# A hybrid decoder step in fp32: the last up pair's stores and difference through GpSimd, and the order of the first down loads

## The chip, the cores and the metric

One core of a Trainium2 chip runs the whole program in one launch. Its engines are TensorE (PE), VectorE (DVE), ScalarE (ACT), GpSimd (POOL) and SyncE (SP), which issues the DMAs. The metric is device time in microseconds; the kernel before has a median of 2629.21 us over 3 runs (2625.51 to 2635.08).

## The reference

One layer of a decoder trunk for 2048 prompt tokens and 64 sample tokens at width 1024: a mixer (gated DeltaNet heads beside sliding-window attention), and then the gated ConvFFN, of which only the end matters here:

```python
h = _rmsnorm(x, norm_ffn_w[i]) * (1 + sc2) + sh2
u = jnp.einsum('bld,df->blf', h, ffn_w_up[i])            # 1024 -> 2 x 2816
u_c, n_f_buf = _causal_dwconv(u, f_buf, ffn_conv_w[i])   # 3 taps along the tokens
gate, up = jnp.split(u_c + ffn_conv_b[i], 2, axis=-1)
x = x + g2 * jnp.einsum('blf,fd->bld', jax.nn.silu(gate) * up, ffn_w_down[i])
...
y = _rmsnorm(x, final_norm_w)
```

All of it is fp32. The results are the normed tokens and the states.

## The kernel before

A product in fp32 is done as three matmuls on halves: each operand is split into a high part (a cast on ACT) and a low part (a subtraction on DVE), and high x high, high x low and low x high are added up in PSUM. So every weight tile and every token tile costs a load, a cast and a subtraction before PE can use it. In the names, `wr` is a raw weight tile, `wh` and `wl` its parts; `th` and `tl` are the parts of a token tile.

**The end of up.** The 2816 gate and up rows are 22 pairs of 128. Pairs 3 to 20 of the second token half run as quarter products in `up_quarters`, and the last, pair 21 (`p == MI - 1`), as plain products at its end. For each pair `elementwise` convolves the gate (`conv`: one pass of ACT, then taps on DVE), takes the Silu on ACT, convolves the up rows, multiplies on DVE into `act` (L1589) and stores it to `act_d` (L1590). `diff_loads` reads an earlier token half back into `d12`, printed as `d`; `diffs` subtracts it from `act` on DVE (L1504), copies the 64 sample columns on ACT (L1521), and stores the result to `E_d` (L1522), all on SP's queue. The last pair's `act`, `d` and stores are the last things that up does.

**Down.** `down_phase` splits 2816 and 1024 and the tokens in two each and makes seven products of sums (`DOWN`), once for each of two column ranges, 14 in all, numbered q. A product has 11 steps i; a step is 4 blocks of output rows by 3 matmuls of 512 columns, 12 matmuls. For each step `get_w` loads, casts and subtracts a weight tile, and `get_t` does it for a token tile. The tokens of product 0 are sums that lie in DRAM (`T1_d`, loaded into the tiles `cT1_i`, which the profile prints as `cT` and the order below as `cT_i`); those of product 1 are `cB`. Product 0 starts while up's last pair is still in its elementwise work.

`ahead` works through the steps in order, some steps in front of PE: `AHEAD` = 3 as a rule, up to `DR` = 6 near the end of a product. `RAWS` = 4 raw weight tiles and `DR` = 6 split ones go round. The last three steps of a product are done block by block, and each block is then added to the residual tile x (`out`), which `load_x` fetches from `x2T` (L1857) at step 1 and, if there are two, at step 5, behind the load that was issued last (`tc.issue_after(fetched[0])`).

What sets the order: the program is recorded, and a scheduler then fixes one order for each engine by its own simulated times, subject to data, memory and `issue_after`. At run time each engine and each queue goes through its list strictly in order. All DMAs of the kernel before stand in SP's list, so a store that waits for DVE holds up every load behind it. SP's DMAs take eight semaphores in turn, and one is issued only when the eighth before it has landed.

Of the kernel before, what the change touches and what calls it, by code (L numbers as in the profile page):

```python
# [18 lines left out]
ALU = mybir.AluOpType  # L19
# [13 lines left out]
MI = 22  # L33
# [9 lines left out]
LH = L // 2  # L43
# [51 lines left out]
def kernel(  # L95
# [5 lines left out]
    nc = tc.nc  # L101
# [8 lines left out]
    def scratch(name, shape):  # L110
        return dp.tile(shape, F32, tag=name, name=name)
# [5 lines left out]
    act_d = scratch("act_d", [MI, P, LT])  # L117
    ws_d = scratch("ws_d", [2 * KH, P, D])
    ts_d = {t: scratch(f"{t}_d", [KH, P, n]) for t, n in (("T1", LT - LH), ("T3", LH), ("E", LT - LH))}
# [274 lines left out]
    def rest(steps):  # L394
        for _ in steps:
            pass
# [1086 lines left out]
    def up_quarters(first, q, h, W, uc, us, pq, sums_done):  # L1483


        c0 = HALVES[1][0][0]
# [4 lines left out]
        sg, act = [hold(t, [P, n]) for t in ("sgq", "actq")]  # L1491
# [4 lines left out]
        d12, d22 = [hold(t, [P, n]) for t in ("d12", "d22")]  # L1496
# [6 lines left out]
        def diffs(p):  # L1503
            sub = lambda out, a, b: nc.vector.tensor_tensor(out[:, :LH], a[:, :LH], b[:, :LH], ALU.subtract)  # L1504
            if p in K1:
                i = K1.index(p)
                sub(sg, d22, d12)
                nc.sync.dma_start(ts_d["T3"][i], sg[:, :LH])
                yield
                yield  # L1510
                sub(d12, d12, act)
                nc.scalar.mul(d12[:, LH:], act[:, LH:], -1.0)
                nc.sync.dma_start(ts_d["T1"][i], d12)
                yield
                return
            i = K2.index(p)
            more = K2[8:][i:i + 1]
            for k in more:
                nc.sync.dma_start(sg, act_d[k, :, c0:])
            sub(d12, act, d12)  # L1520
            nc.scalar.copy(d12[:, LH:], act[:, LH:])  # L1521
            nc.sync.dma_start(ts_d["E"][i], d12)  # L1522
            yield
            yield
            for k in more:
                sub(sg, sg, d22)
                nc.sync.dma_start(ts_d["E"][i + 8], sg)
            yield
# [7 lines left out]
        def conv(m, rb):  # L1536

            w, st = uc["cw"][:, m], b8(o[:, m, 2:18])
            d = pq.tile([P, 3 * 512], F32, tag="cq", name="cq", bufs=1)[:, :n]
            sb = us.tile([P, NB_S, 2 + NT_S], F32, tag="sbq", name="sbq", bufs=2)  # L1540
            tap = lambda out, src, j: nc.vector.scalar_tensor_tensor(out, src, w[:, j:j + 1], out, ALU.mult, ALU.add)
            nc.scalar.copy(rb[:, 0:2], o[:, m, 0:2])
            nc.scalar.activation(d, rb[:, 2:], AF.Identity, bias=uc["cb"][:, m:m + 1], scale=w[:, 2:3])
            nc.gpsimd.tensor_copy(sb[:, :, :2], st)
            nc.scalar.copy(sb[:, :, 2:], b8(rb[:, 2 + np_:]))
            yield d
            tap(d[:, :np_], rb[:, :np_], 0)
            yield
            tap(d[:, :np_], rb[:, 1:1 + np_], 1)
            for j in range(2):  # L1550
                tap(b8(d[:, np_:]), sb[:, :, j:j + NT_S], j)
            nc.scalar.copy(o[:, m, 0:2], rb[:, np_:np_ + 2])
            nc.gpsimd.tensor_copy(st, sb[:, :, NT_S:])
            yield
# [18 lines left out]
        def elementwise(p, ru, rg):  # L1573

            cg = conv(2 * p, rg)
            dg = next(cg)
            yield
            next(cg)
            yield
            next(cg)  # L1580
            nc.scalar.activation(sg, dg, AF.Silu)
            yield
            cu = conv(2 * p + 1, ru)
            du = next(cu)
            yield
            next(cu)
            yield
            next(cu)
            nc.vector.scalar_tensor_tensor(act, du, 2.0, sg, ALU.mult, ALU.mult)  # L1589
            nc.sync.dma_start(act_d[p, :, c0:], act)  # L1590
            yield

        for j in range(RING_T, RING):
# [31 lines left out]
        p = MI - 1  # L1625
        ru, rg = rbs[0][p % 2], rbs[1][0]
        for i, (rb, tags) in enumerate(((rg, "bgc"), (ru, "aub"))):
# [8 lines left out]
            if not i:  # L1636
# [3 lines left out]
                late = elementwise(p, ru, rg)  # L1640
        rest(late)
        rest(diffs(p))


# [30 lines left out]
    def down_phase(ds, dr, pd):  # L1675
# [12 lines left out]
        def w_src(q, i):  # L1688
            t = DOWN[q % ND][0]
            if t[0] == "A":  # L1690
                return I["w_downT"][(K1, K2)[t[2] == "2"][i]][:, (low, high)[t[1] == "2"]]
            return ws_d[KH * (t in ("S1", "S4")) + i, :, (low, high)[t in ("S1", "S3")]]

        def t_src(q, name, i, r):

            at, g = PW * (q // ND), 2 if name in ("B22", "T3") else 1
            if name[0] == "B":
                at += LH * (g == 1)
                return act_d[(K1, K2)[name[1] == "2"][i], :, at + r.start:at + r.stop]
            return ts_d[name][i, :, at + r.start:at + r.stop]  # L1700

        fetched = []

        def load(tag, src, n, most, bufs):

            raw = (ds if tag in IN_DS else dr).tile([P, most], F32, tag=tag, name=tag, bufs=bufs)[:, :n]
            fetched[:] = [nc.sync.dma_start(raw, src).ins]
            return raw

        def halves(pool, tag, raw, most, bufs):  # L1710
            n = raw.shape[1]
            h, l = [pool.tile([P, most], F32R, tag=f"{tag}{s}", name=f"{tag}{s}", bufs=bufs)[:, :n] for s in "hl"]
            nc.scalar.copy(h, raw)  # L1713
            nc.vector.tensor_tensor(l, raw, h.bitcast(F32), ALU.subtract)  # L1714
            return h, l
# [4 lines left out]
        def get_w(q, i):  # L1720
            if (q, i) not in w:
                raw = load("wr", w_src(q, i), D // 2, D // 2, RAWS)
                stay = q == Q - 1 and i >= DR
                w[q, i] = halves(*((dr, f"w{i}") if stay else (ds, "w")), raw, D // 2, 1 if stay else DR)

        def get_t(q, i, r):

            if (q, i, r.start) in t:
                return
            name = DOWN[q % ND][1]  # L1730
            n = r.stop - r.start
            if name in ("T1", "B22"):
                m = wide(q, 1) if name == "T1" else PW
                held[name, i] = load(f"c{name}_{i}", t_src(q, name, i, slice(0, m)), m, big if name == "T1" else PW, 1)
                raw = held[name, i][:, r]
            elif name == "T2":
                raw = dr.tile([P, big], F32, tag="tr", name="tr", bufs=RAWS)[:, :n]
                nc.vector.tensor_tensor(raw[:, :PW], held["B22", i], held["T1", i][:, :PW], ALU.subtract)
                if n > PW:
                    nc.scalar.mul(raw[:, PW:], held["T1", i][:, PW:], -1.0)  # L1740
            else:
                raw = load("tr", t_src(q, "E" if name == "T4" else name, i, r), n, big, RAWS)
                if name == "T4":
                    nc.vector.tensor_tensor(raw, raw, held["T1", i][:, r], ALU.add)
            t[q, i, r.start] = halves(ds, "t", raw, big, DR)
# [12 lines left out]
        def ahead(f):  # L1758

            while done[0] <= min(f, len(queue) - 1):  # L1760
                q, i, r = queue[done[0]]
                get_w(q, i)
                get_t(q, i, r)
                done[0] += 1
# [37 lines left out]
        for q in range(Q):  # L1802
# [61 lines left out]
            for s in (1, 0) if last else (None,):  # L1864
                f = place[q, 0, subs[s].start] if last else f
                cs = [c for c in order if s is None or c[1] == s]
                for i in range(one):
                    ahead(f + reach(i))
                    products(i, cs)
                    if finish and i:  # L1870
                        next(finish, None)
                    if i in (1, 5):
                        load_x()
                    if q == Q - 2 and i >= 2 and i - 2 + DR < KH:
                        get_w(Q - 1, i - 2 + DR)
                ahead(f + one - 1 + DR)
                for c in cs:
                    for i in range(one, KH):
                        products(i, [c])
                    out(*c)  # L1880
                if last:
                    rest(finish or ())
                    r = subs[s]
                    finish = norm(1, r.start, r.stop - r.start, x, sums[1], cols[1], [acc[0, 1], acc[1, 1]], True)
# [13 lines left out]
    SIDE, DR, RAWS, AHEAD = 3, 6, 4, 3  # L1898
# [17 lines left out]
    with ExitStack() as main:  # L1916
# [169 lines left out]
        with ExitStack() as es:  # L2086
            tq = new_pool(es, "tq", side="right")
            W = Quarters(tq)
            q = token_quarters(h, tq)
# [17 lines left out]
    with ExitStack() as es:  # L2107
        ds = new_pool(es, "ds", side="right")
        dr = new_pool(es, "dr")
        down_phase(ds, dr, new_pool(es, "pd", space=PSUM))  # L2110
# [94 lines left out]
```

## Time and profile before

| | |
|---|---|
| median of 3 runs | 2629.21 us (2625.51 to 2635.08) |
| the profiled execution | 2624.72 us |
| its span | 2622.9 us |
| mean granted clock of TensorE in it | 0.996 |
| DMA | 427.62 MB, all on one queue, mean 163 GB/s |
| down phase in the profile | from 2152.67 us to the end |

A group's row reads: line, engine, operation, written tile <- read tiles, shape, count, then behind the bar the busy time and the mean of one in ns, and behind the second bar the idle time of the engine just before these instructions with what ended it. A row of a timeline begins with start and duration in us; in brackets stands the idle time before it. `SPq` is a DMA issue in SP's queue. A row of the windows gives, for one stretch, its length, the busy time of PE, its weight loads, DVE, ACT and POOL with their counts, then the granted clock, the busy share of the DMA engines and GB/s. In the chain of waits each row is start, duration, and what the end of the program hung on in that time.

### The profile page before, as it was taken

How to read it: one execution, taken by the hardware profiler on the slowest of the kernel's cores; microseconds unless marked ns; L12 is line 12 of the kernel's file. 1: busy time of each engine (PE TensorE's matmuls, PEld its weight loads, DVE VectorE, ACT ScalarE, POOL GpSimd, SP SyncE). 2: the span in 40 equal slices, each digit the busy share in tenths (PEclk: the TensorE clock that was granted, in tenths of full speed). 3: DMA queues.
4: the chain of work that ended last, by engine and by line, in shares of the span. 5: the costliest groups of instructions: out<-in, count | busy, mean ns of one | idle time of the engine just before them, and what ended most of it. 6: DMA issues, size and time to landing. Idle time of an engine off the chain costs nothing.

```text
span 2622.9 us, 45390 instructions
## 1 busy us (share of the span) xinstructions
PE 2553.1 (97%) x16424; PEld 2216.3 (84%) x16424; DVE 1840.1 (70%) x3633; ACT 1288.9 (49%) x3140; POOL 795.7 (30%) x708
## 2 busy tenths in 40 slices
PE   6999999999999999999999999999999999999998
PEld 5677888888888787777877789999999997888998
DVE  6475579896544687788768665886777675687676
ACT  5464365554343455555544353654555554454453
POOL 2064143334232322233121123345565520022022
PEclk9999999999999999999999999999999999999999
DMA  7787554343556353333345266325555447676454
GB/s 274 252 296 270 155 144 120 98 121 83 125 187 204 116 136 90 106 103 90 85 141 203 95 209 222 116 73 166 169 168 180 167 162 273 210 243 201 144 192 135
DMA packets 315820, 427.62 MB, mean 163 GB/s; under 512 B 82211, under 2 KB 206212, under 8 KB 315332
## 3 DMA queue, kind: packets, MB, share of 16 engines
q1 hardware_dynamic: 315596, 424.73, 50.9%
q8 instruction: 129, 2.11, 0.3%
q14 instruction: 95, 0.78, 0.1%
HBM read 305.07 MB, written 120.57 MB: 162 GB/s over the span
## 4 chain that ended last, share of the span: by engine, by line
PE 74%; DVE 10%; DMA 7%; ACT 3%; issue 2%; POOL 2%; SPq 1%; POOLq 0%; DVEq 0%; ACTq 0%
PE up_ps L365 17%; PE dn_ps L1825 16%; PE in_ps L365 12%; PE op_ps L365 5%; PE uq_b L1611 5%; PE uq_c L1611 2%; PE uq_u L1611 2%; PE uq_g L1611 2%; PE pv_ps L1033 1%; DVE ev L573 1%; PE uq_a L1611 1%; DMA mt<-mixd 1%; PE as_ps L996 1%; PE u_ps L811 1%; DVE w_lo L357 1%
## 5 line engine op out<-in xcount | busy, mean ns | idle before, releaser
L365 PE MATMUL in_ps<-hi,w_hi 128*128 128x512 f32 (+2 forms) x880 | 318.1, 364 | 4.7 <-DVE ev L629 2.1
L365 PE MATMUL in_ps<-lo,w_hi 128*128 128x512 f32 (+2 forms) x880 | 314.7, 358 | 1.5 <-DVE lo L297 1.1
L365 PE MATMUL up_ps<-hi,w_hi 128*128 128x512 f32 (+2 forms) x808 | 314.3, 389 | 1.5 <-ACT sg L568 1.5
L365 PE MATMUL up_ps<-lo,w_hi 128*128 128x512 f32 (+2 forms) x808 | 313.5, 388 | 1.9 <-DVE lo L297 1.9
L365 PE MATMUL in_ps<-hi,w_lo 128*128 128x512 f32 (+2 forms) x880 | 314.7, 358 | 0.0
L365 PE MATMUL up_ps<-hi,w_lo 128*128 128x512 f32 (+2 forms) x808 | 311.6, 386 | 0.1
L1825 PE MATMUL dn_ps<-th,wh 128*128 128x512 f32 (+2 forms) x796 | 271.4, 343 | 5.1 <-ACT th L1713 5.1
L1825 PE MATMUL dn_ps<-tl,wh 128*128 128x512 f32 (+2 forms) x796 | 272.6, 343 | 0.0
L1825 PE MATMUL dn_ps<-th,wl 128*128 128x512 f32 (+2 forms) x796 | 271.1, 342 | 0.0
L357 DVE TENSOR_TENSOR w_lo<-w_raw,w_hi 128x1024 fp32r<-128x1024 f32 x115 | 145.2, 1263 | 87.4 <-ACT w_hi L356 82.5
L356 ACT CAST w_hi<-w_raw 128x1024 fp32r<-128x1024 f32 x126 | 132.0, 1048 | 139.6 <-PE op_ps L365 52.5
L365 PEld LDWEIGHTS in_ps<-hi,w_hi 128*128 128x128 f32 x880 | 165.4, 189 | 30.8 <-issue 8.6
L365 PEld LDWEIGHTS in_ps<-lo,w_hi 128*128 128x128 f32 x880 | 166.0, 189 | 21.2 <-issue 3.8
L365 PEld LDWEIGHTS up_ps<-lo,w_hi 128*128 128x128 f32 x808 | 152.3, 188 | 37.4 <-issue 10.7
L365 PEld LDWEIGHTS up_ps<-hi,w_hi 128*128 128x128 f32 x808 | 152.3, 188 | 35.9 <-issue 8.6
L365 PEld LDWEIGHTS in_ps<-hi,w_lo 128*128 128x128 f32 x880 | 165.8, 188 | 17.8 <-issue 3.6
L365 PEld LDWEIGHTS up_ps<-hi,w_lo 128*128 128x128 f32 x808 | 152.1, 188 | 31.5 <-issue 5.3
L1713 ACT CAST wh<-wr 128x512 fp32r<-128x512 f32 x149 | 92.2, 619 | 165.2 <-PE dn_ps L1825 110.0
L1825 PEld LDWEIGHTS dn_ps<-th,wh 128*128 128x128 f32 x796 | 150.9, 190 | 21.1 <-ACT th L1713 5.5
L573 DVE SCALAR_TENSOR_TENSOR ev<-rb,cw,ev 128x512 f32<-128x512 f32 (+2 forms) x180 | 140.3, 785 | 38.6 <-ACT ev L566 36.9
L1825 PEld LDWEIGHTS dn_ps<-tl,wh 128*128 128x128 f32 x796 | 151.0, 190 | 16.1 <-DVE tl L1714 0.4
L1825 PEld LDWEIGHTS dn_ps<-th,wl 128*128 128x128 f32 x796 | 151.1, 190 | 15.4
(565 smaller groups left out, 6514.3 us busy)
## 6 DMA issues: line engine op xcount, KB each, us to landing
w_raw<-in_w_upT_dram SPq DMA_DIRECT2D x50, 512.0 KB
wada<-in_w_ada_dram SPq DMA_DIRECT2D x48, 512.0 KB
w_raw<-in_w_inT_dram SPq DMA_DIRECT2D x44, 512.0 KB
wr<-ws_d SPq DMA_DIRECT2D x88, 256.0 KB
w_raw<-in_w_outT_dram SPq DMA_DIRECT2D x34, 512.0 KB
d<-act_d SPq DMA_DIRECT2D x33, 512.0 KB
wr<-in_w_downT_dram SPq DMA_DIRECT2D x66, 256.0 KB
proj<-ev SPq DMA_DIRECT2D x44, 256.0 KB
```

The lines of the kernel that those rows point to most:

```text
L356: nc.scalar.copy(hi, raw)
L357: (eng or nc.vector).tensor_tensor(lo, raw, hi.bitcast(F32), ALU.subtract)
L365: nc.tensor.matmul(ps[:, :n], a[:, k, :], b[:, k, :n], start=first is not False and k == ks[0] and i == 0, stop=last is not False and k == ...
L573: nc.vector.scalar_tensor_tensor(out, src(j), w[:, j:j + 1], out, ALU.mult, ALU.add)
L811: mm = lambda out, a, b, r, c: nc.tensor.matmul(out, a, b, start=True, stop=True, tile_position=(r, c))
L996: nc.tensor.matmul(banks[v][:, 256 * g:256 * g + 256 - P * k0], qs[:, 2 * (g0 + g) + v], t[:, v, :2 - k0].rearrange("p w j -> p (w j)"), s ...
L1033: nc.tensor.matmul(pv_ps[64 * v:64 * v + 64, :], (vprev[0], vt)[half][:, 64 * v:64 * v + 64], PT[v, half], start=half == k0, stop=half == 1)
L1611: nc.tensor.matmul(bk[t][:, :nb], u[:, k], v[:, k], start=new and k == 0 and y == 0, stop=k == KG - 1 and y == 2, skip_group_check=True)
L1713: nc.scalar.copy(h, raw)
L1825: nc.tensor.matmul(acc[m, s][:, :n], w[q, i][a][:, c], th[b][:, v], start=new and i == 0 and y == 0, stop=i == KH - 1 and y == 2, skip_gro ...
```

## The change

```diff
@@ diffs(p), pairs of K2
             for k in more:
                 nc.sync.dma_start(sg, act_d[k, :, c0:])
+            if p == MI - 1:
+                nc.gpsimd.tensor_tensor(d12[:, :LH], act[:, :LH], d12[:, :LH], ALU.subtract)
+                nc.gpsimd.tensor_copy(d12[:, LH:], act[:, LH:])
+                nc.gpsimd.dma_start(ts_d["E"][i], d12)
+                return
             sub(d12, act, d12)
             nc.scalar.copy(d12[:, LH:], act[:, LH:])
             nc.sync.dma_start(ts_d["E"][i], d12)
@@ elementwise
-            nc.sync.dma_start(act_d[p, :, c0:], act)
+            (nc.gpsimd if p == MI - 1 else nc.sync).dma_start(act_d[p, :, c0:], act)
@@ ahead(f)
                 q, i, r = queue[done[0]]
+                if q == 0 and i >= DR:
+                    get_t(q, i, r)
+                    with tc.issue_after(fetched[0]):
+                        get_w(q, i)
                 get_w(q, i)
                 get_t(q, i, r)
@@ the loop over a product's steps
-                    if i in (1, 5):
+                    if i in ((1, 5) if q else (5,)):
                         load_x()
```

For the last pair the two stores (128x1088 fp32 each, 557 KB), the difference (128x1024) and the copy (128x64) go from SP, DVE and ACT to POOL. For product 0 the weight loads from step 6 on are issued behind the token load of their step, and the residual tile is fetched at step 5 instead of step 1. The calls of `get_w` and `get_t` that follow in `ahead` find these tiles made and do nothing.

The scheduler's order of SP around the end of up, before, from the fourth token tile on (`cT_i` is the token tile of step i of product 0, `wr` a weight tile, `x` the residual tile):

```order
L1707 DMA cT_3_22506<-T_d 128x512
L1707 DMA wr<-ws_d 128x512 x6
L1590 DMA act_d<-actq 128x1088
L1522 DMA E_d<-d_18602 128x1088
L2106 DMA out_ffn_conv_dram<-vout 128x684
L1501 DMA d_18602<-act_d 128x1024
L1590 DMA act_d<-actq 128x1088
L1522 DMA E_d<-d_18602 128x1088
L1707 DMA cT_4_22530<-T_d 128x512
L1857 DMA x_22548<-x2T 128x4x512
L1707 DMA cT_5_22556<-T_d 128x512
L1707 DMA cT_6_22580<-T_d 128x512
```

and now:

```order
L1712 DMA cT_3_22506<-T_d 128x512
L1712 DMA wr<-ws_d 128x512 x2
L1595 DMA act_d<-actq 128x1088
L1527 DMA E_d<-d_18602 128x1088
L2115 DMA out_ffn_conv_dram<-vout 128x684
L1501 DMA d_18602<-act_d 128x1024
L1712 DMA cT_4_22530<-T_d 128x512
L1712 DMA cT_5_22554<-T_d 128x512
L1712 DMA cT_6_22572<-T_d 128x512
L1712 DMA wr<-ws_d 128x512
L1712 DMA cT_7_22596<-T_d 128x512
L1712 DMA wr<-ws_d 128x512
```

The second `act_d` and `E_d` stores, those of the last pair, are gone from SP; four of the six weight loads in a row have moved behind tokens 6 to 9, and x behind the weights of step 9. The stores stand in POOL's order now, behind its last copies of up; its next rows are sums of squares of down's products:

```order
L1549 COPY sbq<-vout 128x8x2
L1558 COPY vout<-sbq 128x16
L1595 DMA act_d<-actq 128x1088
L1521 TENSOR_TENSOR d_18602<-actq,d_18602 128x1024
L1522 COPY d_18602<-actq 128x64
L1523 DMA E_d<-d_18602 128x1088
L1301 TENSOR_TENSOR dsum_23548<-dsum_23548,sq 128x512 x7
```

They are the first DMAs of the program on POOL. The tile of the fourth residual load lies where `act` was, so that load now waits for POOL's first store.

DVE, from the last pair's convolution of the up rows on, before:

```order
L1541 SCALAR_TENSOR_TENSOR cq<-sbq,vcw,cq 128x64 x2
L1589 SCALAR_TENSOR_TENSOR actq<-cq,sgq 128x1088
L1504 TENSOR_TENSOR d_18602<-actq,d_18602 128x1024
L1714 TENSOR_TENSOR wl<-wr,wh 128x512
L1714 TENSOR_TENSOR tl<-cT_4_22530,th 128x512
L1714 TENSOR_TENSOR wl<-wr,wh 128x512
L1714 TENSOR_TENSOR tl<-cT_5_22556,th 128x512
```

and now:

```order
L1546 SCALAR_TENSOR_TENSOR cq<-sbq,vcw,cq 128x64 x2
L1594 SCALAR_TENSOR_TENSOR actq<-cq,sgq 128x1088
L1719 TENSOR_TENSOR tl<-cT_4_22530,th 128x512
L1719 TENSOR_TENSOR tl<-cT_5_22554,th 128x512
L1719 TENSOR_TENSOR tl<-cT_6_22572,th 128x512
L1719 TENSOR_TENSOR wl<-wr,wh 128x512
L1719 TENSOR_TENSOR tl<-cT_7_22596,th 128x512
```

The difference and the weights of step 6 no longer stand between the last product and `tl` of step 4.

PE at step 4 of product 0, with the tiles' numbers (22532 and 22533 are `th` and `tl` of step 4, the `dn_ps` are the four blocks), before:

```order
L1825 MATMUL dn_ps_22459<-th_22532,wh_22526 128x512
L1825 MATMUL dn_ps_22459<-tl_22533,wh_22526 128x512
L1825 MATMUL dn_ps_22459<-th_22532,wl_22527 128x512
L1825 MATMUL dn_ps_22460<-th_22532,wh_22526 128x512
L1825 MATMUL dn_ps_22460<-tl_22533,wh_22526 128x512
L1825 MATMUL dn_ps_22460<-th_22532,wl_22527 128x512
```

and now:

```order
L1834 MATMUL dn_ps_22459<-th_22532,wh_22526 128x512
L1834 MATMUL dn_ps_22460<-th_22532,wh_22526 128x512
L1834 MATMUL dn_ps_22458<-th_22532,wh_22526 128x512
L1834 MATMUL dn_ps_22457<-th_22532,wh_22526 128x512
L1834 MATMUL dn_ps_22459<-tl_22533,wh_22526 128x512
L1834 MATMUL dn_ps_22459<-th_22532,wl_22527 128x512
```

The four matmuls that need only `th` now come first, so `tl` is asked for four matmuls into the step; the other steps keep the old order.

## The prediction

> **What bounds the kernel now.** I read the page first, then who TensorE (PE) waits for, the chain that ended last, and the timelines around the one large wait.
>
> ```profile
> span 2622.9 us, 45390 instructions
> ...
> PE 2553.1 (97%) x16424; PEld 2216.3 (84%) x16424; DVE 1840.1 (70%) x3633; ACT 1288.9 (49%) x3140; POOL 795.7 (30%) x708
> ...
> L1825 PE MATMUL dn_ps<-th,wh 128*128 128x512 f32 (+2 forms) x796 | 271.4, 343 | 5.1 <-ACT th L1713 5.1
> ```
>
> PE is busy for 97% of the span, so an edit gains only where PE stands still. The down projection's matmuls (L1825) have one idle time, 5.1 us, ended by a cast of ACT. The profiled execution took 2624.72 us, 1.8 us more than its span, and lies 4.5 us below the median of the runs shown, 2629.21 us. I work out the sum against it and take the difference over to the median.
>
> The chain of waits says what led up to that cast (start, us, what):
>
> ```profile
> 2161.66 1.30 DVE actq L1589
> ...
> 2162.98 1.24 DVE d L1504
> ...
> 2164.27 0.32 SPq L1522
> ...
> 2164.68 3.46 DMA cT<-T_d
> ...
> 2168.17 0.63 ACT th L1713
> ...
> 2168.84 31.21 PE dn_ps L1825 x124
> ```
>
> The load of down's fifth token tile (step 4, cT) was asked for only at 2164.68, when the last up pair's product was done on DVE (2162.96), its difference too (2164.22), and SP had issued the store of that (2164.27). SP's own timeline shows the order:
>
> ```profile
> 2137.98 8.27 SPq L1707 DMA_DIRECT2D wr<-ws_d  x6
> ...
> 2152.36 0.32 SPq L1522 DMA_DIRECT2D E_d<-d  x1
> 2153.99 0.34 SPq L2106 DMA_DIRECT2D out_ffn_conv_dram<-vout  x1
> 2155.15 0.32 SPq L1501 DMA_DIRECT2D d<-act_d  x1
> 2162.97 0.32 SPq L1590 DMA_DIRECT2D act_d<-actq  x1
> ```
>
> From 2155.5 to 2162.97 SP stood at one store that waits for DVE, and all of down's loads stood behind it. This is waiting in a queue, not lack of bandwidth: DMA moved nothing in 2160 to 2161 and 391 GB/s in 2175 to 2176 (last two columns of the windows; the one ahead of them is PE's granted clock).
>
> ```profile
> 2160.00:2161.00 1.00, 1.00 (x6) 0.84 (x5) 0.91 (x1) 0.00 (x0) 0.00 (x0) 1.00 0.00 0
> ...
> 2167.00:2168.00 1.00, 0.00 (x0) 0.00 (x0) 0.00 (x0) 0.00 (x0) 0.00 (x0) 0.81 0.98 326
> ...
> 2173.00:2174.00 1.00, 1.00 (x4) 0.72 (x4) 1.00 (x3) 1.00 (x3) 0.00 (x0) 0.50 1.06 391
> ...
> 2175.00:2176.00 1.00, 1.00 (x6) 0.82 (x5) 1.00 (x3) 1.00 (x3) 0.00 (x0) 1.00 1.07 391
> ```
>
> The same rows show a second price: the clock falls during the wait and is 0.50 for some 7 us. PE's timeline has both:
>
> ```profile
> 2152.67 0.40 PE L1825 MATMUL dn_ps<-th,wh 128*128 128x512 f32 x1
> ...
> 2163.38 0.39 PE L1825 MATMUL dn_ps<-th,wl 128*128 128x512 f32 x1
> 2168.84 0.80 PE L1825 MATMUL dn_ps<-th,wh 128*128 128x512 f32 x1 [5.08 <-ACT th L1713]
> ...
> 2174.42 0.42 PE L1825 MATMUL dn_ps<-th,wh 128*128 128x512 f32 x1
> ```
>
> Steps 0 to 3 are 48 matmuls; from the first start to the last, 10.71 us over 47 gaps, 0.228 us each. The next was due at 2163.61 and came at 2168.84: **5.23 us**. The next 12 took 5.58 us where 2.74 is normal: **2.84 us** of half clock. Together **8.07 us**.
>
> **The change part by part.**
>
> *Store of the last pair, its difference, copy and store to GpSimd (POOL).* Two issues leave SP, 1.24 us leaves DVE, a 64-column copy leaves ACT. SP now goes from the load of d (2155.15) to step 4's token tile at about 2155.5, nine microseconds earlier. Ahead in the transfers are E_d's store, the state output and that load, three transfers where before there were two stores; so I keep the 3.46 us and say landed by 2159.0, and by 2160 if it takes a microsecond more.
>
> ```profile
> 2157.00 1.26 ACT L1543 ACTIVATE cq<-rbu,vcb,vcw 128x1088 f32<-128x1088 f32 x1
> ```
>
> ACT is free from 2158.26, so th is cast by about 2159.7 to 2160.7, before PE wants it at 2163.61. What is late next is tl: it stands behind the product on DVE, ends at 2162.96, and takes one of DVE's subtractions, 0.7 us, so 2163.7. PE's order now asks for four th products first, so tl is due at 2163.61 + 4 x 0.228 = 2164.52. **0.8 us to spare (in the old order, with tl second, 0.1); the wait goes whole, and with it the half clock: 8.07 us.**
>
> *Work added to POOL.* The subtraction there has a row of its own shape (behind the bar: busy us, mean ns):
>
> ```profile
> L357 POOL TENSOR_TENSOR w_lo<-w_raw,w_hi 128x1024 fp32r<-128x1024 f32 x11 | 26.9, 2442 | 55.4 <-ACT w_hi L356 43.1 <-DMA mt<-mixd 12.3
> ```
>
> What POOL and DVE do to each other shows in three more (start, us):
>
> ```profile
> 2119.13 0.69 DVE L1472 TENSOR_TENSOR rl<-rawu,rh 128x512 fp32r<-128x512 f32 x1 [1.71 <-ACT rh L1471]
> ...
> 2121.40 1.29 POOL L1472 TENSOR_TENSOR rl<-S,rh 128x512 fp32r<-128x512 f32 x1 [3.72 <-ACT rh L1471]
> ...
> 2121.49 1.75 DVE L1472 TENSOR_TENSOR rl<-rawg,rh 128x512 fp32r<-128x512 f32 x1
> ```
>
> A subtraction of DVE that takes 0.69 us alone took 1.75 us when one of POOL had begun 0.09 us before it: it ended 0.55 us after POOL did. So POOL's 2.44 us will hold up DVE's next subtractions once. tl of step 4 is released with the product on DVE itself, while POOL has first to take the product's signal and issue a store, so I put the block behind it: tl of step 5 then ends by 2163.7 + 2.44 + 0.7 = 2166.8, due at step 5's second matmul, 2163.61 + 13 x 0.228 = 2166.57. **Cost 0 to 0.3 us, I take 0.1.** Steps 6 and later have more: w of step 6 is third in DVE's row from there, 2168.2, due at 2169.5.
>
> No DMA of POOL is in this trace, so its issue is bounded by SP's 0.32 us and by POOL's longest operation, 7.04 us:
>
> ```profile
> L1097 POOL TENSOR_TENSOR S<-S,cdecS 128x4096 f32<-128x4096 f32 x1 | 7.0, 7044 | 9.0 <-DMA ws_d<-suv 9.0
> ...
> 2270.48 0.43 SPq L1857 DMA_DIRECT2D x<-x2T  x1
> ...
> 2278.19 1.30 POOL L1301 TENSOR_TENSOR dsum<-dsum,sq 128x512 f32<-128x512 f32 x1 [124.23 <-ACT sq L1300]
> ...
> 2316.27 0.32 SPq L1707 DMA_DIRECT2D tr<-E_d  x1
> ```
>
> I take a value near SP's, and either end costs nothing: POOL has 124 us without work, the residual load at 2270.48 takes over the product's memory, and the difference is read in the eighth of E's loads, at 2316.27. That cover is over 100 us long. The Trainium skill, page "DMA: Bandwidth & Descriptors", section "Anatomy of one DMA — SWDGE (gpsimd) path", prices such a transfer at 2.0 us and 1 us per 436 KB; by it the store, 557 KB, would be done 3.3 us after its issue and the sum would stay as it is.
>
> *Weights from step 6 on behind their tokens, residual load from step 1 to step 5.* Before, six weight loads (2137.98) went out early; four of them now stand in SP's queue among the tokens. Ten loads of 256 KB from tokens 4 to weights 9 at 391 GB/s are 0.67 us each, so weights 6 land near 2161 and weights 9 near 2165, due at 2169.1 and about 2175. The residual tile (1 MB, 2.7 us) follows by 2168 and is wanted after step 10, not before 2176. POOL's two stores, 1.1 MB, take 2.8 us of the same bandwidth. **Nothing, with 4 us or more to spare;** had they stayed early they would have cost nothing either.
>
> Sum: 2624.72 - 8.07 + 0.1 = 2616.8 us for an execution like the profiled one; at the median, 2629.21 - 8.0 = **2621 us**.
>
> **The rivals.**
>
> 1. *POOL's subtraction begins ahead of step 4's tl.* That tl would end at 2162.98 + 2.44 + 0.7 = 2166.1 instead of 2164.52: 1.6 us of PE's time. And a short gap is enough for the half clock, as an earlier place shows:
>
> ```profile
> 609.95 0.68 PE L811 MATMUL u_ps<-inv,Y 64*64 64x64 f32 x8 [2.67 <-DVE Y L859]
> ```
>
> ```profile
> 613.00:614.00 1.00, 1.00 (x5) 1.00 (x4) 1.00 (x5) 0.00 (x0) 0.00 (x0) 0.50 0.00 1
> ...
> 615.00:616.00 1.00, 1.00 (x7) 1.00 (x7) 0.93 (x5) 0.85 (x2) 0.00 (x0) 1.00 1.37 311
> ```
>
> There the clock was halved for about 3 us, some 1.5 us of work. Gain 8.1 - 1.6 - 1.5 = 5.0 to 6.5 us: 2623 to 2624. Against it: DVE has tl queued right behind its own product, and POOL a store ahead of its subtraction. Chance 0.17.
>
> 2. *The half clock is not there in most executions*, so only the wait comes back: 5.2 us, 2624. For it: one trace is one execution. Against it: the gap of 2.67 us above was enough. Chance 0.12. The Trainium skill, page "TensorE: Matmul & The Clock Gate", section on the clock gate, has the clock fall after a whole idle window of about 3.4 us that runs on its own phase; by that rule a gap of 5.1 us would hold such a window in about half of the executions. The trace does not agree that a whole one is needed.
>
> 3. *The wait moves to steps 5 to 10*, since ten loads and two stores now crowd the stretch that was free: half of the 8 us or all of it returns, 2625 to 2629. For it: SP issues a load only when the eighth before it has landed. Against it: 4 us to spare. Chance 0.07.
>
> 4. *Slower:* POOL's first DMA of the program holds the product's memory, and the residual load of 2270.48, by then at about 2262, waits for it with every later load of SP behind it. Three steps, 12 x 0.228 = 2.7 us each, are split ahead, so PE waits from a store that lands after 2270, and the change is slower by 0.3% only if that is after 2286, 123 us after its issue: 2637 and more. Nothing in the trace is like it: SP's loads behind its two stores of that size landed within 3.46 us. With it I count what I do not see. Chance 0.04.
>
> That leaves **0.60** for the forecast. The order of the instructions leaves no room for a change that does nothing: step 4's load stands ahead of the last pair's store.
>
> **How the numbers follow.** About 0.3%, 7.9 us, is what a measurement of this kernel tells from no change, and my 8.0 us lie on that line: with 1.5 us instead of 2.84 us of half clock the forecast gives 6.6. So of its 0.60 I put 0.36 on faster and 0.24 on within; the rivals 1 to 3 are within, but for 0.02 of luck. Faster 0.38, within 0.58, slower 0.04. The runs of before reach from 3.7 us below their median to 5.9 above. So the range: 2621 - 6 = 2615, and rival 1 or 2 with as much above, 2624 + 6 = 2630.
>
> **What would show it.** Right: the L1825 groups without the 5.1 us, the clock at 1.00 from 2160 to 2180, SP's token load of step 4 near 2155.5, POOL with a store, a subtraction of 2.4 us and a second store after 2163, and one DVE subtraction there of about 3 us. Wrong: a new wait of L1825 for tl (rival 1) or for a load (rival 3), or a residual load that waits near 2262 (rival 4).

## The result and the profile after

| | before | changed |
|---|---|---|
| median | 2625.48 us (2618.54 to 2635.08, 10 runs) | 2616.45 us (2613.15 to 2620.78, 10 runs) |
| profiled execution, its span | 2624.72 us, 2622.9 us | 2613.15 us, 2611.2 us |
| down, from its first matmul to the end of the span | 2152.67 to 2622.9: 470.23 us | 2149.09 to 2611.2: 462.11 us |

The ratio of the runs is 0.9963, with a 95% interval from 0.9952 to 0.9973. The change makes the kernel 0.37% faster, some 9.7 us (7 to 12.6). The 8.1 us by which down is shorter lie inside that interval.

The page of the changed kernel (engine totals, the three groups of down's matmuls, and the DMA queues):

```profile
span 2611.2 us, 45384 instructions
...
PE 2546.3 (98%) x16424; PEld 2213.2 (85%) x16424; DVE 1841.7 (71%) x3632; ACT 1290.2 (49%) x3139; POOL 802.5 (31%) x712
...
q0 software_dynamic: 288, 1.11, 0.1%
...
L1834 PE MATMUL dn_ps<-tl,wh 128*128 128x512 f32 (+2 forms) x796 | 271.5, 341 | 0.0
L1834 PE MATMUL dn_ps<-th,wh 128*128 128x512 f32 (+2 forms) x796 | 269.9, 341 | 0.0
L1834 PE MATMUL dn_ps<-th,wl 128*128 128x512 f32 (+2 forms) x796 | 268.8, 341 | 0.0
```

No group of down's matmuls waits any more; before, `dn_ps<-th,wh` had 5.1 us. The new queue q0, with 1.11 MB, is POOL's two stores. The chain of waits runs through PE from down's beginning for 185 us (start, us, what):

```profile
2149.25 185.01 PE dn_ps L1834 x816
```

SP's timeline shows why. Step 4's token is the first of the three `cT` at 2151.64, issued right behind the load of `d`. The queue first stands still behind 2158.22, when all of product 0's tokens are out; the next row, step 10's weights, goes at 2163.96:

```profile
2151.23 0.32 SPq L1501 DMA_DIRECT2D d<-act_d  x1
2151.64 1.36 SPq L1712 DMA_DIRECT2D cT<-T_d  x3
...
2158.22 0.32 SPq L1712 DMA_DIRECT2D cT<-T_d  x1
2163.96 0.32 SPq L1712 DMA_DIRECT2D wr<-ws_d  x1
```

ACT's timeline has the casts, `th` of steps 4 and 5 first; DVE's has the last product and then the subtractions `tl`:

```profile
2155.83 1.27 ACT L1718 CAST th<-cT 128x512 fp32r<-128x512 f32 x2 [1.48 <-DMA cT<-T_d]
```

```profile
2157.76 1.29 DVE L1594 SCALAR_TENSOR_TENSOR actq<-cq,sgq 128x1088 f32<-128x1088 f32 x1
2158.96 4.37 DVE L1719 TENSOR_TENSOR tl<-cT,th 128x512 fp32r<-128x512 f32 x3
```

POOL's timeline has the moved work:

```profile
2159.36 0.80 POOL L1595 DMA_DIRECT2D act_d<-actq  x1 [8.98 <-DVE actq L1594]
2160.18 2.42 POOL L1521 TENSOR_TENSOR d<-actq,d 128x1024 f32<-128x1024 f32 x1
...
2163.08 0.58 POOL L1523 DMA_DIRECT2D E_d<-d  x1 [0.31 <-POOL d L1522]
```

PE's timeline: step 4 begins at 2160.02, 10.93 us after down's first matmul, and asks for `tl` at 2160.92.

```profile
2149.09 0.40 PE L1834 MATMUL dn_ps<-th,wh 128*128 128x512 f32 x1
...
2160.02 1.07 PE L1834 MATMUL dn_ps<-th,wh 128*128 128x512 f32 x4
2160.92 0.39 PE L1834 MATMUL dn_ps<-tl,wh 128*128 128x512 f32 x1
```

The half clock is gone with the wait. Before, it lasted from 2167.6 to 2174.4, which is 2164.0 to 2170.9 on this execution's clock; the windows show a granted clock of 1.00 there (the column ahead of the last two), and PE busy throughout:

```profile
2162.00:2168.00 6.00, 6.00 (x28) 4.95 (x28) 5.54 (x8) 1.50 (x4) 1.34 (x3) 1.00 1.04 411
2168.00:2174.00 6.00, 6.00 (x28) 4.99 (x27) 4.06 (x6) 4.08 (x7) 0.00 (x0) 1.00 1.06 392
```

The first cast of `th` begins 4.2 us before step 4. Of the three `tl`, which take 1.89 us where POOL does no subtraction beside them (e3 below), the row is 4.37 us long: 2.5 us are lost beside POOL's subtraction.

**Where the 11.7 us between the two spans come from.** 8.12 us lie in down. The other 3.58 lie ahead of it, in work that both kernels do in the same order but for four weight loads; the difference is there before those loads (the last `act_d` store but two is issued at 2126.51 before and at 2122.92 now). That part differs as much between executions of one order (2151.97 and 2158.95 us up to down's first matmul in two kernels below, e1 and e7). So single executions are compared below by the length of down, and whole times by their medians.

### The profile page after: what moved, and what is told of

It reads as the page before. It is cut to its first block, busy times and chain, and to the rows that moved or that the text cites. A ratio compares the mean times of both kernels' runs of the same rounds, so it can differ in the third digit from the quotient of the medians.

```text
span 2611.2 us, 45384 instructions
## 1 busy us (share of the span) xinstructions
PE 2546.3 (98%) x16424; PEld 2213.2 (85%) x16424; DVE 1841.7 (71%) x3632; ACT 1290.2 (49%) x3139; POOL 802.5 (31%) x712
## 3 DMA queue, kind: packets, MB, share of 16 engines
q0 software_dynamic: 288, 1.11, 0.1%
## 4 chain that ended last, share of the span: by engine, by line
PE 76%; DVE 9%; DMA 7%; POOL 3%; issue 2%; ACT 2%; SPq 1%; POOLq 0%; DVEq 0%; ACTq 0%
PE up_ps L365 19%; PE dn_ps L1834 17%; PE in_ps L365 12%; PE op_ps L365 4%; PE uq_b L1616 4%; PE uq_c L1616 2%; PE uq_u L1616 2%; PE uq_g L1616 2%; PE pv_ps L1033 1%; DVE ev L573 1%; PE uq_a L1616 1%; PE as_ps L996 1%; PE u_ps L811 1%; DMA rawu<-in_w_upT_dram 1%; PE z_ps L811 1%
```

## The experiments

Eight kernels were run. "Down" is the length from its first matmul to the end of the span, "wait" the idle time of down's matmul groups, "half clock" the length of the stretch at 0.50 behind the wait at step 4. The last columns compare the runs with those of before: the changed kernel's with the ten runs above, the others' with 35 runs (medians 2625.55 and 2625.58 us). "Theory Q" and its rivals are worked out in the expectations, which are set off from the text.

| kernel | down | wait | half clock | median | ratio, 95% |
|---|---|---|---|---|---|
| before | 470.23 | 5.1 | 6.8 | | |
| changed | 462.11 | 0.0 | none | 2616.45 | 0.9963 (0.9952 to 0.9973) |
| e1: stores and difference alone | 470.73 | 6.9 | 6.8 | 2627.09 | 1.0007 (0.9997 to 1.0017) |
| e2: order of loads alone | 469.72 | 5.4 | 3.4 | 2627.72 | 1.0006 (0.9998 to 1.0015) |
| e7: changed, weights' order put back | 470.35 | 5.5 | 6.8 | 2626.64 | 1.0004 (0.9994 to 1.0013) |
| e6: changed, residual tile at step 1 | 463.24 | 1.0 | none | 2617.99 | 0.9974 (0.9963 to 0.9984) |
| e3: difference and copy put back | 463.12 | 0.6 | none | 2619.84 | 0.9975 (0.9965 to 0.9986) |
| e4: both stores put back on SP | 469.72 | 5.7 | 6.8 | 2626.82 | 1.0003 (0.9992 to 1.0014) |
| e5: stores on ScalarE, nothing on POOL | 464.35 | 1.4 | none | 2621.61 | 0.9986 (0.9978 to 0.9995) |
| e8: only step 10's weights moved | 464.48 | 2.1 | none | 2620.60 | 0.9985 (0.9976 to 0.9995) |

**The theory** (Q below): the wait was SP's list standing at an instruction that needs the last product, with step 4's token load behind it. **The rivals**: that the loads' order paid, or DVE's relief, and, against my own prediction, whether the weights' move was needed at all.

### e1 and e7: the weight loads where they were

e1 is the kernel before with the first two parts of the diff (the last pair's difference, copy and stores); e7 differs from the changed kernel by this alone:

```diff
-                if q == 0 and i >= DR:
-                    get_t(q, i, r)
-                    with tc.issue_after(fetched[0]):
-                        get_w(q, i)
```

> Only the last pair's two stores, difference and copy go to GpSimd; weights and residual tile are asked for as before. In SP's list the weight load of step 10 then stands ahead of step 4's token load; it needs a raw weight tile that DVE frees with the weights of step 6, and that subtraction stands behind the last product on DVE. Theory Q (a queue stops at its first instruction that cannot go): SP stops at that weight load until about 0.7 us after the product, step 4's token is asked for some 8 us later than in the changed kernel, TensorE waits 4 to 5 us at step 4 and then has about 7 us of half clock; down takes 469 to 470 us from its first matmul to the end of the span (470.2 before, 462.1 changed), and the time is within 1.5 us of the kernel before. Theory P (the prediction's statement that the early weight loads would have cost nothing): no wait of over 0.5 us at step 4, down 462 to 463 us, 8 to 9 us faster than before, like the changed kernel.

> The changed kernel with the weights' order put back (six weight loads ahead of the tokens), the residual tile still at step 5. Theory Q: like the kernel with the stores alone, the weight load of step 10 stops SP until DVE has done the weights of step 6: wait of 4 to 5 us at step 4, half clock about 7 us, down 469 to 470 us, within 1.5 us of before. Theory P: no wait, down 462 to 463 us, 8 to 9 us faster.

Theory Q, both times: nothing is gained. SP's timeline of e1, and DVE's:

```profile
2154.65 0.32 SPq L1501 DMA_DIRECT2D d<-act_d  x1
2163.07 0.32 SPq L1712 DMA_DIRECT2D wr<-ws_d  x1
2163.48 0.38 SPq L1712 DMA_DIRECT2D cT<-T_d  x1
```

```profile
2161.15 1.29 DVE L1594 SCALAR_TENSOR_TENSOR actq<-cq,sgq 128x1088 f32<-128x1088 f32 x1
2162.36 1.28 DVE L1719 TENSOR_TENSOR wl<-wr,wh 128x512 fp32r<-128x512 f32 x2
```

The store is gone from SP, and SP stands still all the same, from 2155.0 to 2163.07, this time at a weight load, that of step 10. It goes when DVE ends the first of the two `wl`, step 6's, which frees the raw tile that it needs and stands behind the product. Step 4's token follows at 2163.48, and PE pays as before, with a second wait of 0.95 us at step 5, behind the residual load. The waits are longer than the 4 to 5 us expected:

```profile
2151.97 0.40 PE L1830 MATMUL dn_ps<-th,wh 128*128 128x512 f32 x1
...
2168.97 2.07 PE L1830 MATMUL dn_ps<-th,wh 128*128 128x512 f32 x4 [5.92 <-ACT th L1718]
...
2174.39 1.20 PE L1830 MATMUL dn_ps<-th,wh 128*128 128x512 f32 x4 [0.95 <-ACT th L1718]
```

e7's timeline is the same picture, with the residual load out of the way: SP stands from 2161.5 to 2169.65 at the weight load, and PE waits 5.5 us once.

### e2: the order of the loads alone

The kernel before with the last two parts of the diff (the weight loads and the residual tile).

> Only the order of loads: weights from step 6 on behind their tokens, residual tile at step 5; the last pair's stores, difference and copy stay on SP, DVE and ScalarE. Theory Q: SP still stops at the store of the last product ahead of step 4's token load, so the wait (5.2 us) and the half clock (2.8 us) stay: down 469.5 to 470.5 us, time within 1.5 us of before. Rival W (the loads' order is what paid, the stores did not matter): wait under 1 us, down 462 to 463 us, 8 to 9 us faster.

Theory Q again. SP's timeline of e2: the token load stands behind the two stores as before.

```profile
2157.26 0.32 SPq L1501 DMA_DIRECT2D d<-act_d  x1
2165.08 0.32 SPq L1590 DMA_DIRECT2D act_d<-actq  x1
2166.37 0.32 SPq L1522 DMA_DIRECT2D E_d<-d  x1
2166.78 1.86 SPq L1707 DMA_DIRECT2D cT<-T_d  x3
```

By the medians e2 is 2.2 us slower than before, where at most 1.5 was expected; the interval of its ratio, 0.9998 to 1.0015, includes 1.

So each half of the change gives nothing, and both together 8.1 us. There are two stops that end about when the last product does, but the kernel before has only the stores ahead of step 4's token. Its load of step 10's weights stands behind the tokens of steps 4 to 9, on SP's timeline of before:

```profile
2169.05 0.38 SPq L1707 DMA_DIRECT2D wr<-ws_d  x1
```

In e1 the same load stands ahead of the token: with the stores off SP, the scheduler made a new order. The second stop came with the first half of the change.

### e8: one weight load moved

```diff
-                if q == 0 and i >= DR:
+                if q == 0 and i == KH - 1:
```

> The changed kernel, but of the weight loads only that of step 10 stands behind its token; those of steps 6 to 9 go out early as before. Theory Q says that this one load alone stopped SP: step 4's token is asked for right behind the load of d, before the last product. DVE then has the weights of steps 6 and 7 between the product and step 4's tl, and tl comes third, where GpSimd's subtraction (2.4 us, from about 1.1 us after the product) held DVE up in the changed kernel: tl ends about 4 us after the product, due 1.5 us after it: a wait of 2 to 3 us ended by DVE's tl, with up to 2.8 us of half clock: down 464 to 468 us, 2.5 to 6 us faster than before. If the token is still asked for behind the last product, theory Q is wrong about the load, and down is 469 us or more.

It is that one load. SP's timeline of e8 has the tokens right behind the load of `d`, and down and the time come out as expected:

```profile
2156.19 0.32 SPq L1501 DMA_DIRECT2D d<-act_d  x1
2156.60 3.02 SPq L1712 DMA_DIRECT2D cT<-T_d  x6
```

What is left is a wait for `tl`, on DVE's, POOL's and PE's timelines:

```profile
2162.70 1.29 DVE L1594 SCALAR_TENSOR_TENSOR actq<-cq,sgq 128x1088 f32<-128x1088 f32 x1
2163.91 1.28 DVE L1719 TENSOR_TENSOR wl<-wr,wh 128x512 fp32r<-128x512 f32 x2
2165.11 3.72 DVE L1719 TENSOR_TENSOR tl<-cT,th 128x512 fp32r<-128x512 f32 x2
```

```profile
2165.12 2.38 POOL L1521 TENSOR_TENSOR d<-actq,d 128x1024 f32<-128x1024 f32 x1
```

```profile
2154.22 0.40 PE L1834 MATMUL dn_ps<-th,wh 128*128 128x512 f32 x1
...
2168.28 0.50 PE L1834 MATMUL dn_ps<-tl,wh 128*128 128x512 f32 x1 [2.07 <-DVE tl L1719]
```

DVE does two subtractions before POOL's begins. The next is held up for its length. In the changed kernel that is `tl` of step 6, which has time; here two weights stand ahead, the third is `tl` of step 4, and PE waits 2.07 us. Early weights can cost in two places: on SP's list (e1, e7) and on DVE's (here, where down is 2.4 us longer than in the changed kernel).

### e4: both stores on SP, the difference still on POOL

```diff
-                nc.gpsimd.dma_start(ts_d["E"][i], d12)
+                nc.sync.dma_start(ts_d["E"][i], d12)
...
-            (nc.gpsimd if p == MI - 1 else nc.sync).dma_start(act_d[p, :, c0:], act)
+            nc.sync.dma_start(act_d[p, :, c0:], act)
```

> The changed kernel with both stores of the last pair on SP; difference and copy stay on GpSimd, weights stay behind their tokens. Theory Q: SP stops at the store of the product ahead of step 4's token load as before, and then at the store of the difference, which GpSimd ends later (2.4 us) than DVE did (1.24 us): the token is asked for 1.2 to 2 us later than before, TensorE waits 6.3 to 7.3 us, half clock 3.4 to 7 us long; down 470 to 472.5 us, 0 to 2.5 us slower than before. Rival G (taking the difference off DVE pays by itself): down under 467 us, 3 us faster than before or more.

The rival falls: with the difference off DVE and the loads in the new order, the time is that of before. SP's timeline of e4 shows both stops:

```profile
2157.01 0.32 SPq L1501 DMA_DIRECT2D d<-act_d  x1
2164.84 0.32 SPq L1595 DMA_DIRECT2D act_d<-actq  x1
2167.47 0.32 SPq L1523 DMA_DIRECT2D E_d<-d  x1
2167.88 1.83 SPq L1712 DMA_DIRECT2D cT<-T_d  x3
```

The wait, 5.7 us, is shorter than I expected. The token was issued 3.04 us behind the store of the product where before it was 1.71, 1.3 us later as expected, but its cast began 3.4 us after its issue (2171.29) where before it was 3.5, and the product itself came 0.6 us earlier against down's first matmul (store issues at 9.66 and 10.30 us after it).

### e3: the difference on DVE again, the stores still on POOL

```diff
             if p == MI - 1:
-                nc.gpsimd.tensor_tensor(d12[:, :LH], act[:, :LH], d12[:, :LH], ALU.subtract)
-                nc.gpsimd.tensor_copy(d12[:, LH:], act[:, LH:])
-                nc.gpsimd.dma_start(ts_d["E"][i], d12)
-                return
...
-            nc.sync.dma_start(ts_d["E"][i], d12)
+            (nc.gpsimd if p == MI - 1 else nc.sync).dma_start(ts_d["E"][i], d12)
```

> The changed kernel with the last pair's difference on DVE and the copy on ScalarE again; both stores stay on GpSimd. Step 4's token is asked for early as in the changed kernel. But DVE then does the difference (1.24 us) between the last product and step 4's tl, and TensorE's order has tl second again. Theory (the prediction's 0.1 us to spare in the old order, less the difference): tl ends 1.24 + 0.7 us behind the product where it is due 0.9 us behind it: a wait of about 1.1 us at step 4, ended by DVE's tl, no GpSimd hold-up of DVE; down 463 to 464.5 us, some 7 us faster than before. Rival H (what the change wins is that DVE and SP together are relieved, so that the difference alone costs the whole wait): a wait of over 4 us, down above 468 us.

DVE's and PE's timelines of e3:

```profile
2167.74 1.23 DVE L1504 TENSOR_TENSOR d<-actq,d 128x1024 f32<-128x1024 f32 x1
2168.88 1.89 DVE L1714 TENSOR_TENSOR tl<-cT,th 128x512 fp32r<-128x512 f32 x3
```

```profile
2157.68 0.40 PE L1829 MATMUL dn_ps<-th,wh 128*128 128x512 f32 x1
...
2169.62 0.50 PE L1829 MATMUL dn_ps<-tl,wh 128*128 128x512 f32 x1 [0.57 <-DVE tl L1714]
```

A wait of 0.57 us for `tl`, about half of what I expected, and three `tl` in 1.89 us with no subtraction of POOL beside them; rival H falls. By down's length, 463.12 against 462.11 us, what left DVE and ACT is worth 1 us; the other 7 us come with the stores off SP and the order of the loads.

### e5: the stores on ScalarE's queue

Like e3, but with `nc.scalar` for `nc.gpsimd` at both stores.

> Both stores of the last pair on ScalarE's queue, difference on DVE, copy on ScalarE, weights behind their tokens; GpSimd is left out. SP is as free as in the changed kernel. ScalarE stops in its turn at the store of the difference, with the cast of step 4's th behind it: difference 1.25 us after the product, two issues of some 0.4 us, th 0.6 us, so th ends about 2.0 to 2.5 us after the product, due 0.6 us after it: a wait of 1.4 to 2 us, ended by ScalarE's th, no half clock or a short one: down 464 to 466 us, 4.5 to 6.5 us faster than before. If any queue but SP's would do, no wait: down 462 to 463 us.

ACT's timeline of e5: ACT stands at the second store until DVE's difference is there, and the casts with it; PE waits 1.06 us for `th`, less than the 1.4 to 2 expected, and 0.23 for `tl`.

```profile
2166.84 0.35 ACTq L1590 DMA_DIRECT2D act_d<-actq  x1
...
2168.16 0.33 ACTq L1522 DMA_DIRECT2D E_d<-d  x1
2168.53 1.66 ACT L1713 CAST th<-cT 128x512 fp32r<-128x512 f32 x3 [1.05 <-DVE d L1504]
```

In each of these runs the store stopped the queue that it stood in; on POOL nothing urgent of down stands behind it. SP was not as free as expected: it stood at a later token load from 2163.6 to 2169.61, without a wait of PE for it. The runs give e5 3.7 us (1.3 to 5.8) over before, where down's length gives 5.9; what else it costs in other executions is open.

### e6: the residual tile at step 1 again

```diff
-                    if i in ((1, 5) if q else (5,)):
+                    if i in (1, 5):
```

> The changed kernel with the residual tile fetched at step 1 again: its 1 MB load stands between the token loads of steps 4 and 5. Both theories: no wait at step 4. The load takes 2.7 us of bandwidth, step 5's token lands by about 2163 on the clock of the changed kernel's profile, needed at 2162.8, so at most 1 us of wait at step 5: down 462 to 463.2 us, 7.5 to 9 us faster than before. If instead the move of the residual tile was needed, a wait of 2 us and more at step 5 and half clock behind it: down 465 us and more.

No wait at steps 4 and 5, though the residual load stands between their tokens. There are two short waits later, which the changed kernel does not have, on PE's timeline of e6:

```profile
2180.99 0.50 PE L1834 MATMUL dn_ps<-th,wh 128*128 128x512 f32 x1 [0.53 <-ACT wh L1718]
...
2184.51 0.47 PE L1834 MATMUL dn_ps<-th,wh 128*128 128x512 f32 x1 [0.51 <-DVE x L1289]
```

By one execution its move is worth 1 us; by the medians, 1.5 us apart with intervals that overlap, it can't be told from nothing.

## Why the prediction was right, and where it was not

**The wait and the half clock: right, in mechanism and size.** The prediction took 5.23 + 2.84 = 8.07 us; down became 8.12 us shorter. Its median, 2621 us, started from 2629.21, the three runs shown; ten runs of the kernel before give 2625.48, and less 8.0 that is 2617.5 beside the measured 2616.45. That the measured time still lies in the range, near its lower end of 2615, is owed to the range's width and not to its middle. The prediction held a gain under 7.9 us for likelier (0.58) than one above it (0.38), for fear of a smaller half clock; the runs give 9.7 us.

**The size of the half clock is one execution's.** Five profiled executions had the long wait, and all five the half clock, so rival 2 falls. But down's length less 462.11 and less the waits leaves 3.0 us for it before, and 1.7 to 2.7 in e1, e2, e4 and e7. The 8.07 and the 8.12 us both come from the one execution of before, so that they agree to 0.05 us is in part luck: with 1.7 to 2.7 us the sum would have been 6.9 to 7.9.

**Step 4's token: right.** Issued at 2151.64, which is 2155.2 with the 3.58 us by which this down began earlier; the prediction said 2155.5. On that clock `th` began at 2159.4, 4.2 us after the issue, where 3.46 us were kept for the load and a microsecond more was allowed, and in time for the expected end between 2159.7 and 2160.7; `tl` began at 2162.5 and, at 0.6 us each, ended at 2163.2, where 2163.7 was expected and 2164.52 needed.

**POOL holding up DVE: the size right, the place one subtraction off.** POOL's subtraction took 2.42 us against 2.44, and DVE lost 2.5. POOL needed 0.80 us for its first store's issue, not SP's 0.32, so DVE had done two `tl` and the third, step 6's, was held. It cost nothing where 0.1 was allowed. e8 shows the price where the held subtraction is needed: rival 1's wait, 2.07 us, without half clock behind it.

**The weights: the step that failed.** "Nothing, with 4 us or more to spare" holds for the loads as moved. The end of that sentence, "had they stayed early they would have cost nothing either", is wrong: in e1 and e7 the weights that stay early cost the whole gain. I asked when the loads would land and not what each waits for before it can be issued. The kernel's own counts say it: with four raw tiles and the loads up to step 9's early, that of step 10 needs step 6's tile, which DVE frees behind the last product, and in e1 and e7 the scheduler's order has that load ahead of step 4's token. In the order of before it stands behind, but early weights are not free even so: in e8, with step 10's behind its token and those of steps 6 to 9 early, down takes 2.4 us more than in the changed kernel. The sum stood, since the change moves all of these loads.

**The stores' own cover: right.** POOL's stores landed 7.3 and 6.1 us after their issue, with the transfers full beside them (411 GB/s in the windows above), where the prediction worked out 3.3 us; the cover of over 100 us hid that. Rivals 3 and 4 show nowhere: down's groups have no wait.

## What to carry to other kernels

A load that comes late for no lack of bandwidth stands behind something in its queue; before you take that away, ask of each instruction between it and the load what it needs, and ask it again of the new order, since a scheduler may put in its place another one that waits for the same thing, and then neither repair alone gains anything. Move a store that waits for compute to a queue with nothing urgent behind it (here POOL, not ACT). Where POOL and DVE share work, see which of DVE's instructions falls beside POOL's and whether it has time.

## What the runs showed of the hardware

- **Half clock comes in pieces of 3.4 us.** Windows of e2 (the column ahead of the last two is the granted clock) and of e1:

```profile
2170.00:2171.00 1.00, 0.04 (x1) 0.04 (x1) 0.06 (x1) 0.62 (x1) 0.00 (x0) 0.88 1.03 385
...
2174.00:2175.00 1.00, 1.00 (x5) 0.84 (x4) 0.69 (x1) 0.33 (x2) 0.00 (x0) 0.91 0.99 301
```

```profile
2165.00:2166.00 1.00, 0.00 (x0) 0.00 (x0) 0.00 (x0) 0.00 (x0) 1.00 (x2) 0.63 1.02 352
...
2172.00:2173.00 1.00, 1.00 (x5) 0.78 (x5) 0.00 (x0) 0.00 (x0) 0.00 (x0) 0.95 1.01 408
```

  With the clock at 0.50 or 1.00, e2 was at half from 2170.76 to 2174.18, 3.4 us, and e1 from 2165.26 to 2172.10, 6.8 us; before, e4 and e7 had 6.8 too. In e1 the drop came 2.2 us after the wait began (2163.05), in e2 5.0 us after (2165.77). The 2.07 us of e8 brought no drop. The Trainium skill, page "TensorE: Matmul & The Clock Gate", section "What's actually happening", has the clock fall after an idle window of about 3.4 us that runs on its own phase. The length of the pieces agrees with it; an idle stretch of that length was not needed in e1, where PE had been idle for 2.2 us.
- **Issuing a DMA of 557 KB** took POOL 0.80 and 0.58 us in the changed kernel, SP 0.32, and ACT 0.35 and 0.33 in e5.
- **A subtraction of POOL holds up one of DVE for its length.** Three `tl` took 4.37 us beside POOL's 2.42 us in the changed kernel and 1.89 without it in e3; in e8 two took 3.72 us beside its 2.38.
